# Two transformer blocks on one core: the second block's first layer, its context rows taken out of the joint output product and feed-forward

## The chip, the cores and the metric

The kernel runs on one core of a Trainium2 chip. The metric is device time in microseconds (us) of one execution, as the median of several. TensorE does the matrix products, VectorE and ScalarE work on tiles in SBUF and PSUM, GpSimd on tiles in SBUF, SyncE (SP) issues the DMA transfers.

## The reference, cut to what matters

Two blocks follow each other on 256 rows of 1024 values. The change lies in the second block. It has two layers; in each, 256 latent rows `x` attend to latents and context, and in the first layer alone the 256 context rows `xc` attend to themselves and get an output product and a feed-forward of their own, with the same weights:

```python
    for l in range(DEPTH):
        last = l == DEPTH - 1
...
        y = _merge(o_lat[0], o_lat[1], o_lat[2], lam, lam_init, g_diff_sub[l]) @ w_out[l]
        x = x + gt_a * _rms(y, g_attn_post[l])
        if not last:
            o_ctx = [_sdpa(qc, kc, vc, s) for (qc, kc, vc), s in zip(cxt, scales)]
            yc = _merge(o_ctx[0], o_ctx[1], o_ctx[2], lam, lam_init, g_diff_sub[l]) @ w_out[l]
            xc = xc + cgt_a * _rms(yc, g_attn_post[l])
        hf = _rms(x, g_ffn_pre[l]) * (1.0 + sc_f) + sh_f
        x = x + gt_f * _rms(_swiglu(hf, w_ffn_gate[l], w_ffn_up[l], w_ffn_down[l]), g_ffn_post[l])
        if not last:
            hfc = _rms(xc, g_ffn_pre[l]) * (1.0 + csc_f) + csh_f
            xc = xc + cgt_f * _rms(_swiglu(hfc, w_ffn_gate[l], w_ffn_up[l], w_ffn_down[l]), g_ffn_post[l])
```

The shifts, scales and gates (`sh_a` and so on, the modulation) come from a product of a condition vector with `w_ada[l]`, 24 MB a layer. The second layer needs `xc` only for its keys and values. w_out is 1024x1024, gate and up 1024x2816, down 2816x1024, all in 32 bits.

## The kernel before

**Products.** Every weight goes through `Stream.chunk` (L187 to 208): a load of 1 MB on SP's queue into one of three raw buffers (`wraw`), then in two pieces a rounded copy by ScalarE (`whi`, L204) and what is missing from it (`wlo`, L206), by the engines listed in `s.low` in turn: VectorE alone, or VectorE and GpSimd where the code sets it so. A pair (`whi`, `wlo`) lies in one of two or three pairs of buffers (`s.parts(n)`). The rows are split in the same way, and a product is three matmuls: rounded rows with rounded weights, the rows' low part with rounded weights, rounded rows with the weights' low part. `Stream.tform` (L242) holds the weight stationary and moves the rows; `Stream.nat` and `Stream.tile` (L211, L229) hold 128 rows stationary and move up to 512 weight columns.

**The second block's first layer** (`second`, L2028). The context's projections come first. Then the context's attention runs with the latents' projections as steps beside it (`attention(0, qc, ...)`, with `every` 2 and three PSUM banks for the projections). Then the latents' attention: `attend` (L1619) makes 20 units, each a generator with several steps, and `pipelined` runs them in 26 rounds: pack keys and queries, scores, maximum (VectorE) and exponential (ScalarE), transposes of the weights, product with the values, normalising, transposing back into `m`. It has five PSUM banks for scores and transposes and two for outputs. Before every round, `self.fill("attention 0")` does one step of the modulation (`ada`, L1377: load 1 MB, four matmuls of 32 columns by 512 at L1390, or a step that sorts a finished block); `FILL` (L18) says how many steps are done where. The second layer's modulation, 27 steps with 24 loads, all runs here.

Then `out2` (L1957) and `ffn2` (L1974) take two jobs, latents and context, with seven banks. In the output product and the down product each weight chunk serves four row tiles, in gate and up it moves 512 columns: both jobs' rows. `closing` (L1866) ends each: square sums (L1882), gate (L1884), inverse roots on [128, 1] (`row_rstd`, L387 to 406), sum into `x` or `xc` (L1891), new roots. `mod_norm` and `norm_T` (L1426, L445) turn the rows for the next product: a diagonal of roots (L413), matmuls (L456), scale and shift on VectorE and ScalarE (L465, L466), low parts (L468). `xc` is stored to DRAM (`xcd`, L2099) and loaded again (L2110) for the second layer's projections, whose query products need only `x`.

**Order.** The program's order is only a priority: the build (`schedule_with_timeline_sim=True`) orders each engine's instructions by its own estimate of when they can start.

## Time and profile before

| | us |
|---|---|
| median of 3 runs | 2714.01 |
| lowest, highest run | 2701.88, 2716.73 |
| the profiled execution | 2723.91 |
| its span | 2722.1 |
| its mean granted TensorE clock | 0.966 |

The profile is of one execution, a little slower than the median. Its page gives the busy share of each engine over the span and in 40 slices of 68 us; stretches of the span can be read one by one, with the busy time of each engine, the mean granted clock of TensorE (1.00 is 2.4 GHz, 0.5 is 1.2 GHz) and the mean busy share of the DMA engines. The second block's first layer begins about 1590, the latents' attention 1728, output product 1834, feed-forward 1904, second layer 2268, its attention 2384, its feed-forward 2528. A matmul's duration overlaps its neighbours'; the pace is the distance from start to start.

### The profile page before, as it was taken

To read this page: it belongs to the slowest core of one execution; us is meant where nothing else is said; L and a number is where in the kernel's file an instruction comes from. 1 tells how busy PE (TensorE), PEld (TensorE's weight loads), DVE (VectorE), ACT (ScalarE), POOL (GpSimd) and SP (SyncE) were. 2 spreads that over 40 slices of the span, in tenths; PEclk is the share of its full clock that TensorE was granted. 3 is DMA by queue.
4 is the path that set the end of the run, shared out by engine and by line. 5 is a ranking of instruction groups with operands and counts; after the bars stand their busy time and mean duration, and the time that the engine had idled before them with its cause. 6 is when DMAs were issued, how large, how long until landed. Compare 5 with 4: busy or idle time off the path is not lost. (4 is left out here: it accounts for less than half of the span.)

```text
span 2722.1 us, 38616 instructions
## 1 busy us (share of the span) xinstructions
PE 2612.3 (96%) x15079; PEld 2170.8 (80%) x15079; DVE 1857.5 (68%) x3078; ACT 1503.8 (55%) x2273; POOL 226.5 (8%) x306
## 2 busy tenths in 40 slices
PE   9999999999999999999999889998999997998998
PEld 7789889688888888887888688567888886866997
DVE  5755466688888989888999778476333336674654
ACT  5344355477777777777777545464422223373543
POOL 1000022100000000000000113012000004310000
PEclk9999999999999999999999998899999997987999
DMA  7755574589999999999999732561322332310553
GB/s 238 278 186 186 171 242 140 201 320 358 346 346 349 360 343 358 366 350 361 350 347 362 243 113 90 202 217 55 101 93 93 103 99 64 112 32 32 171 171 124
DMA packets 305645, 590.21 MB, mean 217 GB/s; under 512 B 16196, under 2 KB 118322, under 8 KB 299186
## 3 DMA queue, kind: packets, MB, share of 16 engines
q1 hardware_dynamic: 305458, 587.69, 62.0%
q8 instruction: 120, 1.97, 0.3%
q14 instruction: 67, 0.55, 0.1%
HBM read 584.49 MB, written 3.16 MB: 216 GB/s over the span
## 5 line engine op out<-in xcount | busy, mean ns | idle before, releaser
L206 DVE TENSOR_TENSOR wlo<-wraw,whi 128x1024 fp32r<-128x1024 f32 (+2 forms) x974 | 1126.3, 1203 | 404.4 <-ACT whi L204 378.8
L204 ACT ACTIVATE whi<-wraw 128x1024 fp32r<-128x1024 f32 (+3 forms) x1023 | 990.8, 1032 | 428.0 <-PE bank L238 165.7
L237 PE MATMUL bank<-whi,xe 128*128 128x512 f32 x896 | 356.5, 398 | 1.1 <-ACT whi L204 1.1
L238 PE MATMUL bank<-whi,xe 128*128 128x512 f32 x896 | 353.3, 394 | 0.0
L240 PE MATMUL bank<-wlo,xe 128*128 128x512 f32 x896 | 254.5, 398 | 1.2 <-DVE wlo L206 1.1
L252 PE MATMUL bank<-fhTl,whi 128*128 128x256 f32 (+1 forms) x736 | 226.3, 331 | 1.9 <-POOL fhTl L468 1.9
L251 PE MATMUL bank<-fhTh,whi 128*128 128x256 f32 (+1 forms) x736 | 226.0, 331 | 2.2 <-ACT fhTh L466 2.2
L237 PEld LDWEIGHTS bank<-whi,xe 128*128 128x128 f32 x896 | 168.6, 188 | 42.9 <-ACT whi L204 2.3
L240 PEld LDWEIGHTS bank<-wlo,xe 128*128 128x128 f32 x896 | 166.8, 189 | 41.2 <-DVE wlo L206 4.2
L238 PEld LDWEIGHTS bank<-whi,xe 128*128 128x128 f32 x896 | 169.1, 189 | 37.7
L1217 PE MATMUL my<-whi,fl 128*128 128x512 f32 x448 | 174.7, 391 | 0.0
L1216 PE MATMUL my<-whi,fh 128*128 128x512 f32 x448 | 174.1, 392 | 0.2 <-ACT fh L349 0.2
L206 POOL TENSOR_TENSOR wlo<-wraw,whi 128x1024 fp32r<-128x1024 f32 (+3 forms) x49 | 108.2, 2220 | 606.5 <-PE bank L254 323.7
L252 PEld LDWEIGHTS bank<-fhTl,whi 128*128 128x128 f32 x736 | 138.7, 190 | 15.9 <-POOL fhTl L468 3.4
L251 PEld LDWEIGHTS bank<-fhTh,whi 128*128 128x128 f32 x736 | 138.3, 190 | 16.2 <-ACT fhTh L466 3.7
L254 PE MATMUL bank<-fhTh,wlo 128*128 128x256 f32 (+1 forms) x736 | 137.9, 330 | 0.0
L238 PE MATMUL bank<-whi,ffl 128*128 128x512 f32 x352 | 137.0, 389 | 0.0
L237 PE MATMUL bank<-whi,ffh 128*128 128x512 f32 x352 | 136.7, 389 | 0.0
L1219 PE MATMUL my<-wlo,fh 128*128 128x512 f32 x448 | 133.9, 396 | 0.0
L254 PEld LDWEIGHTS bank<-fhTh,wlo 128*128 128x128 f32 x736 | 114.5, 191 | 12.5
L252 PE MATMUL bank<-hTl,whi 128*128 128x256 f32 (+1 forms) x424 | 108.0, 291 | 2.7 <-DVE hTl L462 2.2
L251 PE MATMUL bank<-hTh,whi 128*128 128x256 f32 (+1 forms) x424 | 108.5, 292 | 2.1 <-ACT hTh L461 2.1
(602 smaller groups left out, 4454.4 us busy)
## 6 DMA issues: line engine op xcount, KB each, us to landing
wraw<-in_odd_exp_w_dram SPq DMA_DIRECT2D x334, 1024.0 KB, 6.9
wraw<-in_w_ada_dram SPq DMA_DIRECT2D x48, 1024.0 KB, 6.3
wraw<-in_even_ffn_w_dram SPq DMA_DIRECT2D x32, 1024.0 KB, 5.1
wraw<-in_w_ffn_gate_dram SPq DMA_DIRECT2D x22, 1024.0 KB, 5.6
wraw<-in_w_ffn_up_dram SPq DMA_DIRECT2D x22, 1024.0 KB, 5.2
wraw<-in_w_ffn_down_dram SPq DMA_DIRECT2D x20, 1024.0 KB, 4.9
wraw<-in_w_in_dram SPq DMA_DIRECT2D x18, 1024.0 KB, 5.4
wraw<-in_odd_w_in_dram SPq DMA_DIRECT2D x16, 1024.0 KB, 6.7
```

The source lines that it names most:

```text
L204: self.k.behind(0, nc.scalar.activation(h[:, at], r[:, at], AF.Copy))
L206: last = eng.tensor_sub(l[:, at], r[:, at], h[:, at])
L237: nc.tensor.matmul(o, xh[:, k0 + k, ts], h[:, k], start=k0 + k == 0, stop=False)
L238: nc.tensor.matmul(o, xl[:, k0 + k, ts], h[:, k], start=False, stop=False)
L240: nc.tensor.matmul(o, xh[:, k0 + k, ts], l[:, k], start=False, stop=k0 + k == K - 1)
L251: nc.tensor.matmul(outs[g], h[:, k, cs], xh[:, k], start=k == 0, stop=False)
L252: nc.tensor.matmul(outs[g], h[:, k, cs], xl[:, k], start=False, stop=False)
L254: nc.tensor.matmul(outs[g], l[:, k, cs], xh[:, k], start=False, stop=k == K - 1)
L1216: nc.tensor.matmul(y[half], fh[:, r0 + r], h[:, r, hs], start=c + r == 0, stop=False)
L1217: nc.tensor.matmul(y[half], fl[:, r0 + r], h[:, r, hs], start=False, stop=False)
L1219: nc.tensor.matmul(y[half], fh[:, r0 + r], l[:, r, hs], start=False, stop=c + r == F // 128 - 1)
```

## The change

The context's output product, closing, norm and feed-forward become a generator of 33 steps, `context_rest`, with chunks of their own: each of these weights is now loaded and split once for the latents and once for the context. Before two of three rounds of the latents' attention one step is made (17 in all), four more behind the latents' output product, the rest behind the latents' feed-forward. The context's matmuls have three PSUM banks of their own from the latents' attention on; that attention keeps three and one for outputs, and every fourth time the modulation's bank; the latents' output product and feed-forward have four. In the context's steps GpSimd takes every other low part. Some tiles of the attention have a buffer less (`tight`), and in the latents' feed-forward two pairs of split buffers are left of three.

The modulation of the second layer leaves the latents' attention: two of its steps go with each of the context's column groups that are done after that attention (14 steps), 13 behind the second layer's attention. `attend` can write its output as a rounded copy and a low part (`put`), which the context's and the second layer's attention do; the second layer's attention leaves the modulation's bank alone. `closing`, `out2` and `ffn2` are written for one job. The context's rows are stored to `xcd` twice (after the output product and at the end), and loaded again for the second sum.

```diff
-    "even norm": 0, "even": 1, "even out": 3, "even ffn norm": 3, "even ffn": 0, "odd norm": 3, "odd": 0, "before router": 0, "router": 7, "norm 01": 0, "norm 00": 0, "latents 0": 0, "attention 0": 1, "out 0": 1, "ffn norm 0": 0, "ffn 0": 0, "layer 1": 0, "norm 10": 0, "norm 11": 0, "latents 1": 0, "out 1": 0, "ffn norm 1": 0, "ffn 1": 0, "end": 0,
+    "even norm": 0, "even": 1, "even out": 3, "even ffn norm": 3, "even ffn": 0, "odd norm": 3, "odd": 0, "before router": 0, "router": 7, "norm 01": 0, "norm 00": 0, "out 0": 0, "ffn norm 0": 0, "ffn 0": 0, "context": 0, "rest of context": 2, "layer 1": 0, "norm 10": 0, "norm 11": 0, "attention 1": 0, "ffn norm 1": 0, "ffn 1": 0, "end": 0,
...
-                    m = self.apool.tile([128, 512], F32, name="m4", bufs=2)
+                    m = self.apool.tile([128, 512], F32, name="m4", bufs=1)
...
-    def attend(self, pool, ps, pp, l, q, kvs, m, beside=None, shared_bank=True):
+    def attend(self, pool, ps, pp, l, q, kvs, m, beside=None, share=6, tight=False):
...
-            if shared_bank and turn[1] % 6 == 0:
+            if share and turn[1] % share == 0:
...
+        def put(k, o, scale=1.0):
+            if not isinstance(m, tuple):
+                nc.scalar.activation(m[:, k], o, AF.Copy, scale=scale)
+                return
+            hi, lo = (z[:, k] for z in m)
+            nc.scalar.activation(hi, o, AF.Copy, scale=scale)
+            nc.vector.scalar_tensor_tensor(lo, o, scale, hi, op0=OP.mult, op1=OP.subtract)
...
-            p = pool.tile([128, 2, nk], F32, name="ap", bufs=4 if nkc == 4 else 5)
+            p = pool.tile([128, 2, nk], F32, name="ap", bufs=5 if nkc < 4 else 3 if tight else 4)
...
-            return pool.tile([128, nkc, T], F32, name="apt", bufs=3)
+            return pool.tile([128, nkc, T], F32, name="apt", bufs=2 if tight else 3)
...
-            nc.scalar.activation(m[:, at + pr], back(on, b), AF.Copy)
+            put(at + pr, back(on, b))
...
-    def closing(self, s, pool, jobs, l, j, store=None):
+    def closing(self, s, pool, x, n, l, j, store=None):
...
+    def gated(self, z, gate, o, junk, ss, c, t):
+        cs = slice(c * 512, (c + 1) * 512)
+        self.nc.scalar.activation(junk, o, AF.Square, accum_out=ss[:, c, t:t + 1])
+        self.nc.vector.tensor_mul(z[:, cs], o, gate[:, cs])
+    def context_rest(self, s, hold, m, out):
+        nc, tc = self.nc, self.tc
+        F = 2816
+        ctx_in = self.i["ctx_2"][0].rearrange("(t p) d -> p t d", p=128)
+        halves = [slice(c * 512, (c + 1) * 512) for c in range(2)]
+        def added(x, ys, ss, junks):
+            r, new = self.row_rstd(ss), self.stats()
+            for t in range(NT):
+                for c, cs in enumerate(halves):
+                    nc.vector.scalar_tensor_tensor(x[:, t, cs], ys[t][:, cs], r[:, t:t + 1], x[:, t, cs],
+                                                   op0=OP.mult, op1=OP.add)
+                    nc.scalar.activation(junks(), x[:, t, cs], AF.Square, accum_out=new[:, c, t:t + 1])
+            nc.sync.dma_start(out, x)
+            return self.row_rstd(new)
+        with tc.tile_pool(reuse_waits="tile", name="cx1", bufs=1, side="right") as pool:
+            xc = pool.tile([128, NT, D], F32, name="cxx")
+            nc.sync.dma_start(xc, ctx_in)
+            gate = self.gate_rows(s, pool.tile([128, D], F32, name="cgate"), 0, 0, 1)
+            w = self.wview(self.dram("w_out_2", 0))
+            ys = [pool.tile([128, D], F32, name="cy", bufs=NT) for _ in range(NT)]
+            ss = self.stats()
+            junk = lambda: pool.tile([128, 512], F32, name="sqj", bufs=1)
+            for c in range(2):
+                banks = [s.bank() for _ in range(NT)]
+                for k0 in range(0, KD, 4):
+                    chunk = s.chunk(w[:, k0:k0 + 4, halves[c]])
+                    for x, o in zip(tiles(m), banks):
+                        s.tile(o, x, chunk, k0, KD)
+                    yield
+                for t, o in enumerate(banks):
+                    self.gated(ys[t], gate, o, junk(), ss, c, t)
+            r = added(xc, ys, ss, junk)
+            hT = self.packs(hold, "c")
+            exhaust(self.mod_norm(s, pool, xc, r, hT, self.g["g_ffn_pre"][0], 0, 1, 1, "cy"))
+            yield
+        w1, w3, w2 = (self.wview(self.dram(f"w_ffn_{a}_2", 0)) for a in ("gate", "up", "down"))
+        with tc.tile_pool(reuse_waits="tile", name="cx2", bufs=1, side="right") as pool:
+            ys = [pool.tile([128, D], F32, name="cy", bufs=NT) for _ in range(NT)]
+            ff, done = [], 0
+            def down(group, evacuate):
+                nonlocal done
+                k = 2 * len(group)
+                xs = tiles([Cat([z[a] for z in group], 0) for a in range(2)])
+                for c, cs in enumerate(halves):
+                    for t, o in enumerate(s.nat(xs, w2[:, done:done + k], c * 512, 512)):
+                        evacuate(ys[t], c, t, o)
+                done += k
+            def summed(y, c, t, o):
+                z = y[:, halves[c]]
+                if done:
+                    nc.vector.tensor_add(z, z, o)
+                else:
+                    nc.scalar.activation(z, o, AF.Copy)
+            for f0 in range(0, F, 256):
+                z = [pool.tile([128, 2, T], F32R, name=a, bufs=3) for a in ("cfh", "cfl")]
+                a, b = banks = [s.bank() for _ in range(2)]
+                for o, w in zip(banks, (w1, w3)):
+                    s.tform([(hT, [o[:, :T], o[:, T:]])], w, f0, 256)
+                    yield
+                sg = pool.tile([128, 2, T], F32, name="ffs", bufs=1)
+                flat = sg.rearrange("p g n -> p (g n)")
+                nc.scalar.activation(flat, a, AF.Silu)
+                nc.vector.tensor_mul(flat, flat, b)
+                self.split(*z, sg)
+                self.fill("rest of context" if self.late else "context")
+                ff.append(z)
+                m = 2 if done else 1
+                if len(ff) > m:
+                    down(ff[:m], summed)
+                    ff = ff[m:]
+                    yield
+            xc = hold.tile([128, NT, D], F32, name="ch")
+            nc.sync.dma_start(xc, out)
+            z = hold.tile([128, 4, 512], F32, name="cl")
+            gate = self.gate_rows(s, z[:, :2].rearrange("p a n -> p (a n)"), 0, 1, 1)
+            ss = self.stats()
+            turn = [0]
+            def junk():
+                turn[0] += 1
+                return z[:, 2 + turn[0] % 2]
+            def last(y, c, t, o):
+                summed(y, c, t, o)
+                self.gated(y, gate, y[:, halves[c]], junk(), ss, c, t)
+            down(ff, last)
+            yield
+            self.context_rms = added(xc, ys, ss, junk)
...
+            ff = self.packs(pool, "ff", F // 128)
+            self.ffn_up(s, pool, hT, w1, w3, ff, 0, F, f"ffn {l}", [norm()])
+            self.fill("end", ADA * (l + 1))
+            return self.closing(s, closed, x, 0, l, 1, store)(ff, w2)
...
-        def attention(l, q, kvs, m, beside=None, every=0, banks=0, steps=None):
-            if not steps:
-                self.fill("end", -(-self.filled // (ADA // 3)) * (ADA // 3))
+        def attention(l, q, kvs, m, project=None, every=0, banks=0, po=2, **more):
             with (tc.tile_pool(reuse_waits="tile", name="att", bufs=1) as pool,
-                  tc.tile_pool(reuse_waits="tile", name="attps", bufs=5 - banks, space=PSUM) as ps,
-                  tc.tile_pool(reuse_waits="tile", name="attpo", bufs=2, space=PSUM) as pp, ExitStack() as more):
-                if not beside:
-                    return self.attend(pool, ps, pp, l, q, kvs, m, steps and (lambda: self.fill(steps)), not steps)
-                more.enter_context(s.banks(banks))
-                s.low = [nc.vector, nc.gpsimd]
-                count = iter(range(1, 100))
-                self.attend(pool, ps, pp, l, q, kvs, m, lambda: next(count) % every == 0 and next(beside, None))
-                exhaust(beside)
-                s.low = [nc.vector]
+                  tc.tile_pool(reuse_waits="tile", name="attps", bufs=7 - banks - po, space=PSUM) as ps,
+                  tc.tile_pool(reuse_waits="tile", name="attpo", bufs=po, space=PSUM) as pp):
+                if not project:
+                    return self.attend(pool, ps, pp, l, q, kvs, m, **more)
+                with s.banks(banks):
+                    s.low = [nc.vector, nc.gpsimd]
+                    count = iter(range(1, 100))
+                    self.attend(pool, ps, pp, l, q, kvs, m, lambda: next(count) % every == 0 and next(project, None),
+                                **more)
+                    exhaust(project)
+                    s.low = [nc.vector]
...
-                    mc = mix.enter_context(tc.tile_pool(reuse_waits="tile", name="mix", bufs=1, side="right")).tile(
-                        [128, KD, T], F32, name="mc")
+                    hold = mix.enter_context(tc.tile_pool(reuse_waits="tile", name="hold", bufs=1, side="right"))
+                    mc = self.packs(hold, "c")
                     with tc.tile_pool(reuse_waits="tile", name="projl", bufs=1) as pool:
                         q = lp.tile([128, NT, self.QW], F32, name="q0")
-                        attention(0, qc, [kv[1]], mc, self.project(s, pool, 0, [(hl, True, kv[0], q)], tabs), 2, 3)
-                m = mix.enter_context(tc.tile_pool(reuse_waits="tile", name="mixl", bufs=1, side="right")).tile(
-                    [128, KD, T], F32, name="m")
-                self.fill("latents 0", 2 * ADA // 3)
-                attention(0, q, kv, m, steps="attention 0")
-            with s.parts(1), s.banks(7), tc.tile_pool(reuse_waits="tile", name="xcp", bufs=1) as xp:
-                xc = xp.tile([128, NT, D], F32, name="xc")
-                nc.sync.dma_start(xc, rows(ctx_in))
-                stats = self.out2(s, xp, [(x, 0, m), (xc, 1, mc)], 0)
-                self.fill("out 0", ADA)
-                stats = self.ffn2(s, xp, [(x, 0), (xc, 1)], stats, 0)
-                nc.sync.dma_start(rows(xcd), xc)
+                        attention(0, qc, [kv[1]], mc, self.project(s, pool, 0, [(hl, True, kv[0], q)], tabs), 2, 3,
+                                  tight=True)
+                banks = mix.enter_context(tc.tile_pool(reuse_waits="tile", name="cbk", bufs=3, space=PSUM))
+                rest = self.context_rest(s, hold, mc, rows(xcd))
+                def context(n):
+                    before, s.psum = s.psum, banks
+                    s.low = [nc.vector, nc.gpsimd]
+                    for _ in range(n):
+                        next(rest, None)
+                    s.psum, s.low = before, [nc.vector]
+                with tc.tile_pool(reuse_waits="tile", name="mixl", bufs=1) as mp:
+                    m = mp.tile([128, KD, T], F32, name="m")
+                    self.late = False
+                    rounds = iter(range(100))
+                    attention(0, q, kv, m, banks=3, po=1, share=4, tight=True,
+                              beside=lambda: context(1 if next(rounds) % 3 else 0))
+                    with s.banks(4), tc.tile_pool(reuse_waits="tile", name="cl", bufs=1) as closed:
+                        r = self.out2(s, closed, x, m, 0, False)
+                        self.late = True
+                        context(4)
+            with s.banks(4), tc.tile_pool(reuse_waits="tile", name="cl", bufs=1) as closed:
+                r = self.ffn2(s, closed, x, r, 0)
+                context(99)
         self.fill("layer 1", ADA + ADA // 3)
...
-                    pre(s, pool, xc, stats[1], h[1], 1, 1)
+                    pre(s, pool, xc, self.context_rms, h[1], 1, 1)
...
-                self.fill("latents 1", ADA + 2 * ADA // 3)
-                attention(1, q, kv, m)
+                attention(1, q, kv, m, share=0)
+                self.fill("attention 1", 2 * ADA)
```

## Rows read from the trace of the kernel before

**Rows 1.** The page: the core's busy line, and the clock in 40 slices.

```profile
PE 2612.3 (96%) x15079; PEld 2170.8 (80%) x15079; DVE 1857.5 (68%) x3078; ACT 1503.8 (55%) x2273; POOL 226.5 (8%) x306
...
PEclk9999999999999999999999998899999997987999
```

**Rows 2.** Busy time in stretches; the columns stand in the first line.

```profile
core 0: us, PE busy (x) PEld busy (x) DVE busy (x) ACT busy (x) POOL busy (x), PEclk, DMA share, GB/s
1728.00:1834.00 106.00, 103.06 (x1006) 62.32 (x1003) 65.08 (x157) 63.60 (x150) 13.97 (x54) 0.98 0.63 231
1880.00:1912.00 32.00, 22.41 (x126) 19.59 (x125) 23.75 (x79) 14.00 (x30) 7.52 (x7) 0.79 0.10 34
1904.00:2268.00 364.00, 363.96 (x1709) 305.81 (x1710) 140.17 (x184) 107.73 (x148) 14.79 (x12) 1.00 0.29 94
2264.00:2312.00 48.00, 28.37 (x127) 24.57 (x126) 35.94 (x121) 19.75 (x41) 19.15 (x12) 0.69 0.20 65
2384.00:2485.00 101.00, 94.91 (x825) 67.92 (x826) 62.26 (x148) 59.26 (x146) 13.39 (x54) 0.76 0.07 22
2528.00:2714.00 186.00, 185.31 (x1308) 174.44 (x1307) 98.19 (x125) 85.04 (x120) 0.52 (x1) 1.00 0.51 165
...
2428.00:2476.00 48.00, 48.00 (x261) 31.52 (x262) 20.88 (x56) 18.34 (x45) 5.82 (x25) 0.51 0.00 1
2272.00:2280.00 8.00, 0.00 (x0) 0.00 (x0) 8.00 (x8) 2.22 (x4) 7.06 (x3) 0.68 0.17 49
```

**Rows 3.** TensorE in order of time, joint feed-forward: ends of two groups of 24.

```profile
2235.14 1.98 PE L254 MATMUL bank<-fhTh,wlo 128*128 128x512 f32 x8
...
2240.58 1.98 PE L254 MATMUL bank<-fhTh,wlo 128*128 128x512 f32 x8
```

**Rows 4.** The chain of waits, second layer's feed-forward: start, length, what.

```profile
2530.03 0.96 PE bank L254 x8
...
2532.91 0.96 PE bank L254 x8
```

**Rows 5.** Instructions by line and shape, 1650 to the end: split pieces.

```profile
L206 DVE TENSOR_TENSOR wlo<-wraw,whi 128x1024 fp32r<-128x1024 f32 x143 | 169.0, 1220 | 156.6 <-ACT whi L204 156.6
L204 ACT ACTIVATE whi<-wraw 128x1024 fp32r<-128x1024 f32 x158 | 158.3, 1051 | 199.1 <-PE bank L252 74.7 <-PE bank L238 66.4 <-issue 52.8
...
L206 POOL TENSOR_TENSOR wlo<-wraw,whi 128x1024 fp32r<-128x1024 f32 x15 | 37.0, 2489 | 398.8 <-PE bank L254 323.7 <-ACT whi L204 75.0
```

**Rows 6.** One line, 1700 to 1834: the modulation's matmuls.

```profile
L1390 PE MATMUL aps<-wraw,cp x192: 592/592/1063, 1718.0 to 1804.1; 128*32 128x512 f32 x192
```

**Rows 7.** TensorE in order of time: one modulation chunk, and products with the identity.

```profile
1724.59 1.07 PE L1390 MATMUL aps<-wraw,cp 128*32 128x512 f32 x8
1725.58 1.15 PE L1693 MATMUL po<-kv,apt 128*64 128x64 f32 x32
...
1835.34 2.94 PE L1421 MATMUL bank<-consts,mod 128*128 128x128 f32 x24 [0.21 <-ACT m L1737]
```

**Rows 8.** The chain of waits, last down product: two groups of 12.

```profile
2661.03 0.91 PE bank L240 x4
...
2663.76 0.91 PE bank L240 x4
```

**Rows 9.** VectorE and GpSimd in order of time, second joint.

```profile
2266.65 0.15 DVE L395 TENSOR_TENSOR ss<-ss 128x1 f32<-128x1 f32 x1
...
2274.95 2.30 DVE L395 TENSOR_TENSOR ss<-ss 128x1 f32<-128x1 f32 x1
2277.17 2.38 DVE L403 SCALAR_TENSOR_TENSOR rstdb<-rstd,rstdv 128x1 f32<-128x1 f32 x1
...
2273.77 5.76 POOL L206 TENSOR_TENSOR wlo<-wraw,whi 128x1024 fp32r<-128x1024 f32 x2
```

**Rows 10.** ScalarE in order of time: the table load ahead of silu.

```profile
1925.10 1.28 ACT L512 ACT_TABLE_LOAD   x1
```

**Rows 11.** Busy time, a stretch of the context's attention beside the latents' projections.

```profile
1664.00:1704.00 40.00, 39.72 (x286) 32.20 (x285) 31.08 (x107) 19.97 (x58) 17.27 (x44) 1.00 0.28 96
```

**Rows 12.** Waits of SP's queue, 2262 to 2320: total, times, longest.

```profile
SPq L2099 <- DVE rstd L399: 9.3, 1, 9.3
...
SPq L2110 <- DMA xcd<-xc: 3.6, 1, 3.6
```

177 lines of the change are left out of this document (55 added, 122 removed).

## The prediction, made before the changed kernel was run

> **What bounds the kernel now.** I read the profile's page first. TensorE is busy 96% of the span and the clock line stands at 9 in nearly every slice [rows 1], so the time is TensorE's work plus the places where it waits or runs at the lower clock. The dips of the clock line lie in the second block, so I then read stage by stage (busy time in stretches). There a stretch's length less busy time times granted clock is what TensorE lost. In the joint feed-forward, 1904 to 2268, it loses nothing (363.96 of 364 us at 1.00) [rows 2]. Between output product and feed-forward it loses 32 - 22.41 x 0.79 = 14.3 us, between feed-forward and the second layer's projections 48 - 28.37 x 0.69 = 28.4 us; one 8 us stretch there has no matmul at all while VectorE is busy for all of it [rows 2]. In the latents' attention (1728 to 1834) it loses 106 - 103.06 x 0.98 = 5.0 us, in the second layer's attention 101 - 94.91 x 0.76 = 28.9 us, most of it from 48 us at clock 0.51, about the 1.2 GHz level [rows 2].
>
> So the two joints are chains of small VectorE, ScalarE and GpSimd steps that all latents and all context rows go through at once, with no matmul left to do. The change puts the context's matmuls there, and into the first layer's attention.
>
> **The change, part by part.** Most of it moves work that TensorE must do anyway; only differences count.
>
> *Narrower products.* Gate and up are computed with the weight stationary. Joint, 24 matmuls of 512 columns take 2240.58 - 2235.14 = 5.44 us [rows 3]. Alone, 24 of 256 columns take 2532.91 - 2530.03 = 2.88 us [rows 4]. There are 22 groups of 128 columns in each of two weights: 44 x (2 x 2.88 - 5.44) = **+14.1 us** on the path. Output and down products have the rows stationary and 512 weight columns moving, one product per row tile before and after: 0.
>
> *Weights loaded and split twice.* w_out is 4 chunks of 1 MB, gate, up and down 11 each: 37 more chunks, each with two more ScalarE pieces (1.05 us) and two low parts, on VectorE 1.22 us or GpSimd 2.49 us [rows 5]. That is 74 x 1.05 = 78 us ScalarE, 37 x 1.22 = 45 us VectorE, 37 x 2.49 = 92 us GpSimd, spread over some 400 us of stages in which these engines are busy 4 to 61% of the time and the DMA engines 29 to 63% [rows 2]. Cover: TensorE's 5.4 to 5.8 us per chunk; if it were gone, a chunk would wait about 3.3 us (two ScalarE pieces, one VectorE piece). 37 more issues stand on SP's queue, and 0 is taken. The latents' feed-forward also loses its third pair of split buffers: a pair comes free in the second half of its chunk, and the next but one needs it a whole chunk later, 5.8 us against 3.3; 0.
>
> *What stands in the latents' attention.* The layer-1 modulation leaves it: 192 records of two passes, four matmuls a chunk, are 24 chunks [rows 6]; one takes 1725.58 - 1724.59 = 1.0 us [rows 7]. So 106 us hold 24 of modulation and 82 of attention and stalls. In come 17 of the context's 33 steps (26 rounds, two of three): output product 8 x 12 matmuls at 2.72/12 us [rows 8] = 21.8 us, norm and gate 40 x 2.94/24 [rows 7] = 4.9, ten weight chunks at 2 x 2.88 = 57.6, the down product of three groups 72 x 2.72/12 = 16.3: 101 us. The stage should take 82 + 101 = 183 us, every us of which leaves a later stage. What mixing costs I have to bound. Below: it hides the stage's 5.0 us of losses. Above: the low parts that GpSimd takes hold VectorE. While GpSimd did two such pieces (5.76 us), VectorE operations of 128x1 took 2.30 and 2.38 us, where the same took 0.15 [rows 9]. Eighteen chunks in the attention bring some 17 full pieces, 17 x 2.49 = 42 us, and the attention's chain runs through VectorE (maxima, reciprocals). Silu among exponentials adds up to 8 table loads of 1.28 us [rows 10]: 10 us. So -5 to +52. Nearest is the stretch where the latents' projections run beside the context's attention with GpSimd on low parts too: 17.27 us of GpSimd in 40, TensorE at 39.72, clock 1.00 [rows 11]. By it nearly all is hidden; for its 3 (not 5) score banks, one output bank and the table loads I take **+5 us**.
> The Trainium skill (ScalarE: Activation LUTs, Rules for kernel authors) says to do all work of one table set before switching, and prices a switch with its drain at about 2.7 us; by that price, were all eight on the path, the term would be 21 us, and the whole 16 us later. Rows 10 show the load alone, 1.28 us; no row shows a drain.
>
> *First joint.* Four context steps follow the latents' output product: three weight chunks, a down product of two groups and four modulation steps, 3 x 5.76 + 10.9 + 4 = 32 us of matmuls against 14.3 lost. The closing chain also has two row tiles instead of four. Bounds 0 and -14.3; **-12**, since the chain's own first matmuls still wait.
>
> *Second joint.* After the latents' last down product 12 steps remain: nine weight chunks and three down products of two groups, 9 x 5.76 + 3 x 10.9 = 84.5 us, and ten modulation steps. Under them the latents' closing and the layer-1 norm of x run. That norm now waits for the modulation's first block, which is filled in with the context's ninth group; 4 x 5.76 + 2 x 10.9 = 45 us of matmuls stand behind that. What is late next is the context's own end: four evacuations, two inverse roots, the sum, store and reload of xcd, norm. The reload queues on SP behind the store, and weights of the projections behind both; before, SP waited 9.3 us for the store's data and 3.6 us for the store [rows 12]. (xcd is now stored and reloaded once more, in the attention and ahead of the context's last down product; there loads queue behind those waits at the same price, under the latents' matmuls: 0.) The cover of the context's end is the latents' query products, which need only x: the rank-256 product (5.8 us), 48 matmuls of 512 columns (10.9) and 60 narrower ones (8): 25 us. So I leave 6 us: **-22 us**, bounds 0 and -28.4.
>
> *Modulation.* Fourteen of its 27 steps run in the context's later steps, 13 (11 chunks) after attention 1, where the build may pull them in. Out of the first layer: **-11 us**. In attention 1 they cost between +11 (all on the path) and 11 - 28.9 = -18 (all hidden, clock kept at 2.4 GHz). The nearest row is the latents' attention with 24 such chunks, at clock 0.98 [rows 2]; but 11 placed late need not keep it: **0**. The rest (merged copies, `sc` and `m4` with one buffer less, packs written directly) comes to under 1 us either way.
>
> Sum: 14.1 + 0 + 5 - 12 - 22 - 11 + 0 = -25.9 us. The profiled execution took 2723.9 us (span 2722.1 and 1.8 around it), 9.9 above the median 2714.0. It would become 2698; against the median, **2688 us**.
>
> **Rivals.** (a) *More is hidden.* The mix hides the stage's own losses (-10 against my +5), the second joint closes fully (-6, the first -2), and attention 1 keeps its clock, say -10: 2660 us. For: rows 11 and the latents' attention at 0.98 in rows 2. Against: the build orders each queue by its own estimate of time, and what comes late holds what stands behind it.
> (b) *The context's end takes the second joint's place.* If its chain of roots, store, reload and norm starts when the x-only products are already spent, the 22 us stay: 2710 us, no difference to be told. For: the chain is as long as the one that now leaves 8 us without a matmul [rows 2]. Against: 25 us of x-only products.
> (c) *Slower: VectorE is held in the attention.* The place is the latents' attention; the price is 42 us of held VectorE and 10 of table loads instead of my 5: 2688 + 47 = 2735 us. It decides from 45 of those 52 us on, that is if nearly every GpSimd piece falls on the maximum, exponential, transpose chain. For: rows 9, and VectorE's 65 us there plus 21 of new low parts and 42 held make 128 of 183, before the context's norm, evacuations and sums. Against: rows 11.
> The Trainium skill (GPSIMD Engine Reference, Key points) warns of this: GpSimd shares its SBUF interfaces with VectorE and contends with instructions that have two SBUF inputs. Rows 9 agree.
>
> **How the numbers follow.** Forecast 0.51 (own range 2674 to 2700), (a) 0.19, (b) 0.19, (c) 0.11. A measurement of this kernel can tell about 0.5%, 13.6 us, so faster means below 2700.4 and slower above 2727.6. Faster is forecast and (a), 0.70; same is (b), 0.19; slower is (c), 0.11. The range takes in most of (a) and (b), leaves (c) out and the far end of (a): 2658 to 2718.
>
> **What would show it.** Right: the stretch of the latents' attention 183 to 190 us at clock near 1; 11 chunks of modulation in attention 1; no stretch of 8 us without a matmul between the latents' last down product and attention 1; latents' feed-forward at 186 us, as the second layer's is now [rows 2]. Wrong: long VectorE entries beside GpSimd low parts with TensorE waiting on the maxima (c); TensorE waiting on the context's roots or on the reload (b); a latents' feed-forward above 190 us, which would mean that two pairs of buffers or the second loading are not free.

## The result, and the profile after

The changed kernel takes 2747.6 us (median of 4 runs, 2743.8 to 2748.6), the kernel before 2715.4 beside it: ratio 1.0123, 95% interval 1.0084 to 1.0163. It is 32 us slower where 26 us faster were forecast; 2747.6 lies outside the range. The profiled execution after took 2748.1 us (span 2746.3), that of before 2723.9, so the two traces show 24 of the 32 us.

The page's busy line and clock line after, which answer to [rows 1]:

```profile
PE 2628.8 (96%) x16039; PEld 2223.0 (81%) x16039; DVE 1926.6 (70%) x3120; ACT 1578.7 (57%) x2359; POOL 301.0 (11%) x326
...
PEclk9999999999999999999999997899999997987999
```

TensorE is as busy as before, with 960 matmuls more, and the clock line dips in the same three places. The stretches after, columns as in [rows 2]:

```profile
1728.00:1923.00 195.00, 187.90 (x1605) 157.17 (x1600) 120.21 (x239) 121.36 (x232) 58.52 (x74) 0.96 0.30 98
1945.00:1983.00 38.00, 37.60 (x262) 31.38 (x261) 30.96 (x74) 19.79 (x34) 16.80 (x9) 1.00 0.72 249
1983.00:2168.00 185.00, 185.00 (x1321) 175.18 (x1320) 94.52 (x112) 84.11 (x117) 0.00 (x0) 1.00 0.58 188
2171.00:2271.00 100.00, 98.36 (x673) 83.47 (x671) 55.62 (x85) 42.89 (x58) 37.05 (x16) 1.00 0.76 256
2268.00:2316.00 48.00, 22.14 (x94) 18.18 (x92) 28.41 (x77) 16.24 (x31) 15.08 (x10) 0.64 0.36 112
2272.00:2280.00 8.00, 0.00 (x0) 0.00 (x0) 7.71 (x7) 3.23 (x6) 7.17 (x4) 0.69 0.68 221
2280.00:2288.00 8.00, 0.00 (x0) 0.00 (x0) 6.91 (x24) 2.72 (x8) 1.72 (x1) 0.50 0.11 40
2392.00:2508.00 116.00, 108.78 (x933) 71.38 (x932) 71.31 (x167) 65.90 (x152) 14.75 (x56) 0.79 0.35 128
```

In their order: the latents' attention with the context's steps in it; the first joint, now full; the latents' feed-forward, full; the rest of the context's feed-forward, nearly full; the second joint, which has two stretches of 8 us without a matmul where [rows 2] have one; the second layer's attention, 15 us longer and still at a low clock. The two joints had been the aim: one is closed, the other is wider than before.

TensorE's waits from the context's last product to the second layer's attention, after (total, times, longest):

```profile
PE bank L456 <- DVE ndg L413: 18.9, 1, 18.9
PE bank L1508 <- ACT sc L1499: 7.7, 2, 6.1
PE bank L252 <- DVE h0l L468: 2.9, 1, 2.9
```

The longest of them before the change, between the feed-forward and the second layer's attention:

```profile
PE bank L456 <- DVE ndg L413: 15.4, 2, 14.7
```

L456 turns `x` for the second layer, with the scaled identity `ndg`. So the wait that was to go has become longer. After, the roots of `x` stood at 2184.6 and the modulation's first block at 2202, 87 us before `ndg`. VectorE in order of time shows where `ndg` stood:

```profile
2277.14 2.30 DVE L395 TENSOR_TENSOR ss<-ss 128x2 f32<-128x2 f32 x1
2279.48 2.27 DVE L397 TENSOR_SCALAR rstdv<-ss 128x2 f32<-128x2 f32 x1
...
2283.57 2.74 DVE L1949 SCALAR_TENSOR_TENSOR ch<-cy,rstd,ch 128x512 f32<-128x512 f32 x4
...
2289.40 0.47 DVE L413 TENSOR_SCALAR ndg<-consts,rstd 128x128 f32<-128x128 f32 x2
```

It stands behind the context's whole closing: gates, first roots, sum (L1949), second roots. So what was to be done under the context's matmuls began only when they and their closing were over.

For the experiments I cut each trace into five stages: A from the end of the latents' first-layer projections to their output product (the latents' attention), B from there to their feed-forward (output product, first joint), C to its last down product, D to the end of the second layer's projections (rest of the context, second joint, projections), E to the second layer's feed-forward. Stage lengths are differences of matmul times of the one profiled execution.

| kernel | median us | ratio to before, interval | A | B | C | D | E |
|---|---|---|---|---|---|---|---|
| before | | | 139.3 | 58.0 | 373.7 | 113.1 | 138.5 |
| after | 2747.6 | 1.0123 (1.0084 to 1.0163) | 231.6 | 59.2 | 188.6 | 221.2 | 152.5 |
| e1 | 2737.8 | 1.0108 (1.0075 to 1.0142) | 232.0 | 59.5 | 188.5 | 218.4 | 145.8 |
| e2 | 2730.0 | 1.0068 (1.0044 to 1.0091) | 225.3 | 58.3 | 188.8 | 218.2 | 145.2 |
| e3 | 2747.2 | 1.0127 (1.0083 to 1.0171) | 231.6 | 59.2 | 188.5 | 221.6 | 152.1 |
| e4 | 2743.5 | 1.0104 (1.0058 to 1.0150) | 260.7 | 59.4 | 192.3 | 204.4 | 142.2 |
| e5 | 2737.2 | 1.0079 (1.0052 to 1.0106) | 232.0 | 59.8 | 188.6 | 214.1 | 152.2 |
| e6 | 2729.4 | 1.0049 (1.0028 to 1.0070) | 225.4 | 58.2 | 188.9 | 211.8 | 151.7 |
| e7 | 2729.0 | 1.0052 (1.0034 to 1.0070) | 232.1 | 60.1 | 188.6 | 220.7 | 135.4 |
| e8 | 2755.3 | 1.0147 (1.0109 to 1.0184) | +30.6 | 60.0 | 188.6 | 213.7 | 135.7 |
| e9 | 2735.2 | 1.0078 (1.0057 to 1.0099) | 231.7 | 59.6 | 188.6 | 222.1 | 143.8 |
| e10 | 2735.8 | 1.0076 (1.0059 to 1.0093) | 230.2 | 59.8 | 188.5 | 211.1 | 143.8 |
| e11 | 2707.8 | 0.9969 (0.9954 to 0.9985) | 225.3 | 58.3 | 188.9 | 208.5 | 134.4 |
| e12 | 2701.2 | 0.9954 (0.9936 to 0.9971) | 225.3 | 58.3 | 188.9 | 201.0 | 132.7 |
| e13 | 2730.2 | 1.0067 (1.0039 to 1.0095) | 229.4 | 59.1 | 188.5 | 220.8 | 135.0 |
| e14 | 2708.0 | 0.9997 (0.9972 to 1.0022) | 230.1 | 58.3 | 188.9 | 198.6 | 139.3 |
| e15 | 2771.7 | 1.0235 (1.0182 to 1.0289) | 132.6 | 49.9 | 192.3 | 360.0 | 149.4 |
| e16 | 2695.0 | 0.9933 (0.9913 to 0.9953) | 224.8 | 58.3 | 188.9 | 201.0 | 133.0 |

(e8: its A begins inside work that was moved; +30.6 is how much later its output product starts than after's, 1953.9 against 1923.3.)

### The profile page after: what moved, and what is told of

It reads as the page before. It is cut to its first block, busy times and chain, and to the rows that moved or that the text cites. A ratio compares the mean times of both kernels' runs of the same rounds, so it can differ in the third digit from the quotient of the medians.

```text
span 2746.3 us, 40908 instructions
## 1 busy us (share of the span) xinstructions
PE 2628.8 (96%) x16039; PEld 2223.0 (81%) x16039; DVE 1926.6 (70%) x3120; ACT 1578.7 (57%) x2359; POOL 301.0 (11%) x326
## 5 line engine op out<-in xcount | busy, mean ns | idle before, releaser
L206 DVE TENSOR_TENSOR wlo<-wraw,whi 128x1024 fp32r<-128x1024 f32 (+2 forms) x1014 | 1187.1, 1216 | 419.7 <-ACT whi L204 387.2
L204 ACT ACTIVATE whi<-wraw 128x1024 fp32r<-128x1024 f32 (+3 forms) x1099 | 1065.8, 1032 | 441.3 <-PE bank L238 172.0
L206 POOL TENSOR_TENSOR wlo<-wraw,whi 128x1024 fp32r<-128x1024 f32 (+3 forms) x85 | 201.7, 2379 | 600.9 <-ACT whi L204 375.7
L252 PE MATMUL bank<-fhTl,whi 128*128 128x256 f32 x704 | 173.0, 284 | 0.9 <-POOL fhTl L468 0.9
L251 PE MATMUL bank<-fhTh,whi 128*128 128x256 f32 x704 | 172.8, 284 | 0.7 <-ACT fhTh L466 0.7
L237 PE MATMUL bank<-whi,ffh 128*128 128x512 f32 x264 | 102.9, 390 | 0.0
L238 PE MATMUL bank<-whi,ffl 128*128 128x512 f32 x264 | 102.7, 389 | 0.0
L254 PE MATMUL bank<-fhTh,wlo 128*128 128x256 f32 x704 | 100.2, 285 | 0.0
```

Of the source, the lines that this page charges most:

```text
L204: self.k.behind(0, nc.scalar.activation(h[:, at], r[:, at], AF.Copy))
L206: last = eng.tensor_sub(l[:, at], r[:, at], h[:, at])
L237: nc.tensor.matmul(o, xh[:, k0 + k, ts], h[:, k], start=k0 + k == 0, stop=False)
L238: nc.tensor.matmul(o, xl[:, k0 + k, ts], h[:, k], start=False, stop=False)
L251: nc.tensor.matmul(outs[g], h[:, k, cs], xh[:, k], start=k == 0, stop=False)
L252: nc.tensor.matmul(outs[g], h[:, k, cs], xl[:, k], start=False, stop=False)
```

## The experiments

**e1: x's norm with scratch of its own.** `xs` is a pool opened ahead of the layer's `proj`:

```diff
-                    pre(s, pool, x, r, h[0], 1, 0)
+                    pre(s, xs, x, r, h[0], 1, 0)
...
-                    tabs = self.tables(pool, 1)
+                    tabs = self.tables(xs, 1)
```

> The scratch of the second layer's norm of x (scaled identity, gains, copies) and its tables get memory of their own instead of memory that the context's sum still reads; nothing else is changed. Theory M (shared memory made x's norm wait for the context's end): the 18.9 us wait of TensorE on the scaled identity behind the context's last down product falls under 4 us, the joint loses 15 to 25 us less, and the ratio to before falls from 1.012 to 1.003 to 1.007 (2722 to 2733 us). Rival E (the context's own end is the chain that decides): the wait only moves to the context's norm behind the query products; total within 6 us of 2747. Rival G (VectorE held by GpSimd's low parts): the scaled identity comes earlier on its queue, but VectorE entries of 2 us stand in its chain all the same; under 8 us won.

TensorE's waits in that part of e1, then VectorE in order of time:

```profile
PE bank L1508 <- ACT sc L1499: 7.7, 2, 6.1
PE bank L251 <- ACT h0h L466: 7.4, 5, 5.9
PE bank L456 <- DVE cy L1993: 4.2, 1, 4.2
PE bank L252 <- DVE h0l L468: 4.0, 1, 4.0
```

```profile
2293.49 0.17 DVE L1429 SCALAR_TENSOR_TENSOR mg<-mod,cols 128x8 f32<-128x8 f32 x1 [1.82 <-DMA xcd<-ch]
2293.57 0.47 DVE L413 TENSOR_SCALAR ndg<-consts,rstd 128x128 f32<-128x128 f32 x2
2293.97 0.41 DVE L468 TENSOR_TENSOR h0l<-xf,h0h 128x256 fp32r<-128x256 f32 x1
```

The 18.9 us wait is gone, so memory had held it: nothing but the place of the scratch was changed. But D is only 2.8 us shorter. The norm's matmuls next wait 4.2 us for a bank that the context's sum still reads (L1993); then `x`'s first low part `h0l` stands in VectorE's queue behind the context's closing, the store of `xcd` and the gains of the context's norm. The wait had three holders, one behind the other, and all three theories had a part; the other 7 us of the 10 are in E (last section).

**e2: no low parts on GpSimd in the context's steps.**

```diff
-                    s.low = [nc.vector, nc.gpsimd]
+                    s.low = [nc.vector]
```
(in `context`)

> The context's weights have all low parts on VectorE, none on GpSimd, in the latents' attention and behind it. Rival G (GpSimd's pieces hold VectorE at the context's end and in the attention): the 2.3 us entries there go, the second joint is 8 to 15 us shorter, ratio 1.006 or less. Theory M: the wait on the scaled identity stays at 13 to 19 us, since only the two holds of some 2 us go; VectorE has some 18 pieces of 1.2 us more in the attention, so the total lies between 5 us less and 10 us more than 2747.

The wait on the scaled identity stays (18.2 us from the context's last product to `x`'s norm), as theory M said; the total fell by more than it allowed. A is 6.3 us shorter, B 0.9, D 3.0, E 7.3. In E nothing was changed; there the stretch at 1.2 GHz is 23.9 us instead of 41.0. e6 against e5 gives the price without that: A 6.6, B 1.6, D 2.3, E 0.5; medians 7.8 us. So GpSimd's pieces cost the change 8 to 10 us, some 6.5 of them in the latents' attention, although VectorE has the more to do without them. The maxima of that attention, which read PSUM, take as long beside these pieces as without them; first after, then in e2 (count, duration in ns, first and last start):

```profile
L1671 DVE TENSOR_REDUCE ast<-sbank x32: 669/688/693, 1740.9 to 1890.8; 128x1 f32<-128x512 f32 x32
```

```profile
L1671 DVE TENSOR_REDUCE ast<-sbank x32: 675/682/692, 1732.1 to 1879.7; 128x1 f32<-128x512 f32 x32
```

Some other VectorE operations in stage A are longer after than in e2; line by line, their mean durations times their counts differ by some 16 us in all, a third of it in VectorE's own low parts (mean 1.46 us against 1.17).

**e3 and e7: the modulation of the second layer's attention, later.** e3 fills one step a round from the ninth on; e7 orders each step behind the last value product as well:

```diff
-                attention(1, q, kv, m, share=0)
-                self.fill("attention 1", 2 * ADA)
+                late = iter(range(100))
+                def step():
+                    if next(late) >= 8:
+                        self.ada_after = self.recent
+                        self.fill("attention 1")
+                        self.ada_after = None
+                attention(1, q, kv, m, share=0, beside=step)
+                self.fill("end", 2 * ADA)
```
(e7; `self.recent` is the last matmul of `weigh`; e3 is without the two `ada_after` lines)

> The modulation steps that stood behind the second layer's attention, and were pulled to its start, stand one in each round from the ninth on. Theory C (they cost their full 11 us because they stand where TensorE is busy, ahead of the stretch at 1.2 GHz): now they fill that stretch; the second layer's attention falls from 116 us to 103 to 109, the 41 us at 1.2 GHz get shorter by at least 15, total 7 to 13 us below 2747. Rival W (they cost what they take wherever they stand, the stretch's clock does not hear of them): attention 114 to 120 us, total within 4 us of 2747, or above it if each chunk takes 2 us at 1.2 GHz.

> e3 left each instruction where it had been; here each modulation step from the ninth round of the second layer's attention on is ordered behind the last value product recorded so far, so that it can't be pulled to the start. Theory C: the stretch at 1.2 GHz in that attention falls from 41 us to 25 or less and the attention from 116 to 104 to 110 us, ratio 1.008 to 1.010. Rival W: 114 to 120 us, ratio 1.011 to 1.014.

e3 tells nothing: the build, for which the program's order is a priority only, put the chunks where they had been. The modulation's matmuls in that attention, after and in e7 (count, duration in ns, first and last start):

```profile
L1390 PE MATMUL aps<-wraw,cp x88: 592/592/618, 2392.2 to 2426.9; 128*32 128x512 f32 x88
```

```profile
L1390 PE MATMUL aps<-wraw,cp x88: 592/612/1062, 2419.7 to 2474.9; 128*32 128x512 f32 x88
```

And that attention in e7 as a stretch, up to its last value product, which answers to the last stretch after:

```profile
2393.00:2492.00 99.00, 93.94 (x936) 60.87 (x935) 70.27 (x168) 66.07 (x152) 13.64 (x56) 0.98 0.44 150
```

The same 11 chunks, 27 to 48 us later: the clock is 0.98 instead of 0.79, the attention takes 99 us instead of 116, E 135.4 instead of 152.5, the median falls by 18.6. E is then shorter than before the change, where it held no chunk (138.5). Theory C holds, and more strongly than it had said. Not all of the 17 us is the chunks' place: e9 and e10, whose edits lie elsewhere, have E at 143.8 with less time at 1.2 GHz (last section), and against them e7 gains 8 us.

**e4, e8, e13: the modulation in the first layer.** e4 puts all 27 steps into the latents' attention again, e8 18 of them into the context's attention; both take the modulation's bank from the scores (`share=0`). e13 puts nine steps between the two attentions and gives up no bank:

```diff
                     m = mp.tile([128, KD, T], F32, name="m")
+                    self.fill("end", ADA + ADA // 3)
                     self.late = False
```

> All 27 modulation steps of the second layer stand in the latents' attention again, one a round, as before the change; the attention gives up the modulation's bank for its scores. Theory C: the second layer's attention is back at 101 to 104 us, the context's rest at 93 to 95, the latents' attention about 24 longer less 6 to 10 that its own idle places give back; total 10 to 18 us below 2747. Rival W (the places in the latents' attention are full with the context's steps): attention longer by 24 or more, total within 5 us of 2747.

> 18 of the 27 modulation steps stand, ordered in the same way, two a round from the sixth round of the context's own attention on (which gives up the modulation's bank for scores), the other nine in the context's rest, none in the second layer's attention. Theory S (the context's attention lost its cover when the modulation left its end: 30.7 us at 1.2 GHz from 1695, 10.2 us before the change): that stretch falls to 15 us or less, the second layer's attention to 100 to 106 us, and the latents' attention starts less than 12 us later than now; total 8 to 18 us below 2747, ratio 1.006 to 1.009. Rival W: 18 chunks cost 16 us or more in their new place, total within 4 us of 2747.

> The changed kernel with the nine steps of the modulation's first block of the second layer (eight chunks) between the context's and the latents' attention, where modulation stood before the change; three chunks are left behind the second layer's attention. Theory S (with the modulation went the cover of that place, 30.7 us at 1.2 GHz from 1695 against 10.2 before): the stretch falls to 20 us or less, from the end of the latents' projections to their output product it takes 229 to 234 us (231.6 now) though eight chunks more are in it, and the second layer's attention is 8 us shorter; ratio 1.008 to 1.010. Rival W (eight chunks cost eight us there too): 238 to 241 us in that part, ratio 1.011 to 1.014.

e4: A is 29.1 us longer with 24 chunks in it, C 3.7, D and E are 27 shorter, and the median falls by 4: rival W. With no chunk in the second layer's attention, E is 142.2. e8: the output product starts 30.6 us later with 16 chunks; TensorE waits 6.8 us for a score bank at the start, and the total is 8 us above after, where neither theory had it. That fewer score banks eat up what the place gains is likely, but no run varies the banks alone. e13 leaves the banks as they are. The stretch with the start of the latents' attention after, then in e13:

```profile
1690.00:1730.00 40.00, 36.08 (x239) 25.65 (x236) 26.07 (x83) 19.25 (x57) 9.91 (x21) 0.62 0.22 79
```

```profile
1690.00:1730.00 40.00, 38.11 (x307) 25.03 (x308) 19.75 (x71) 14.48 (x46) 3.19 (x14) 0.70 0.31 122
```

The 1.2 GHz stretch there is 23.9 us instead of 30.7, and A is 2.2 us shorter with eight chunks more. Eight chunks that elsewhere take 8 us cost nothing here: theory S, a little weaker in the clock than it said (e14, below, is less kind to it). (The median falls by 17 us. In the profiled execution, the trace of which is 23.5 us shorter, 17.5 of them are E's, with three chunks left and 20.5 us at 1.2 GHz; the others lie between 2722.6 and 2741.0.)

**e15: no context step in the latents' attention** (`beside` left out, all 33 steps behind it).

> The changed kernel with no context step in the latents' attention: all 33 behind it (four in the first joint, the rest behind the latents' feed-forward), modulation steps with the same groups as before. Theory X (mixing is worth what the attention loses without it): the attention alone is 82 us of matmuls and loses 20 to 30 us at 1.2 GHz and in waits, the rest of the context takes 101 us more; total 10 to 22 us above 2747. Rival G (the attention pays for the mix in held VectorE and table loads what it gains): total within 5 us of 2747.

The stretch of the latents' attention in e15:

```profile
1690.00:1820.00 130.00, 118.19 (x1101) 85.36 (x1102) 84.67 (x224) 75.80 (x197) 16.57 (x68) 0.86 0.08 26
```

The kernel is 24 us slower than after, a little more than theory X said, but not for its reason. Alone the attention takes 132.6 us; with some 101 us of the context's matmuls in it (the prediction's estimate), 231.6: they cost 99 us, so the mix comes nearly free but hides little of the attention's own losses. (Length less busy time times clock says the same: 28.4 us lost in the stretch above, 231 - 220.04 x 0.90 = 33.0 from 1692 to 1923 after.) The 24 us are lost in D, where TensorE now waits twice for a scaled identity:

```profile
PE bank L456 <- DVE ndg L413: 39.2, 2, 20.4
```

The wait of 20.4 us is new. Behind the latents' last down product stands the context's own first closing (roots, sum, new roots, norm), with no matmul ready, and the clock falls to 0.5 in it. In the kernel after, the attention's matmuls cover this chain. So this is what the mix wins, and it is the part of the change that works. A second reading: alone, without a chunk, A takes 132.6; before the change it took 139.3 with 24 chunks. The modulation had cost some 7 us there, not 24 (the banks differ, so this is rough).

**e5, e6: x's norm ahead of the context's last steps.** The second layer's tiles are laid out behind the latents' feed-forward, and

```diff
+            with s.banks(4):
+                context(5)
+                self.fill("layer 1", ADA + ADA // 3)
+                pre(s, xs, x, r, h0, 1, 0)
+                tabs = self.tables(xs, 1)
+                context(99)
```

> The second layer's norm of x and its tables stand in the program five context steps behind the latents' feed-forward, ahead of the context's last steps, with scratch and banks of their own; the layer's tiles are laid out before the context ends. Theory O (the wait has three holders, one behind the other: the shared scratch, which the first experiment took away, the banks that the context's last products hold, and the place on VectorE's queue behind the context's closing): all are gone, so no matmul waits on the scaled identity of x or on its copies behind the context's last product; from that product to the second layer's attention some 98 to 104 us instead of 121, ratio to before 1.001 to 1.005. Rival E (the context's own end is longer than the products that need x alone): the wait comes back behind the query products, 108 to 115 us, ratio 1.007 to 1.010.

> As e5, and the context's low parts all on VectorE as in e2. If the two prices are separate (GpSimd's pieces cost the latents' attention some 6 us, the order of the norms the joint), the ratio is that of e5 less 0.004 to 0.007, 0.995 to 1.001; if they are one price seen twice, it is that of e5 within 0.002.

TensorE's longest waits from the context's last product on, e5:

```profile
PE bank L1508 <- ACT sc L1499: 13.3, 2, 7.2
PE bank L456 <- DMA xc<-xcd: 6.2, 1, 6.2
PE bank L251 <- DVE cy L1993: 4.2, 1, 4.2
```

Rival E for the most part. `x`'s norm waits for nothing, D is 7.1 us shorter, but 28 us now lie between the context's last product (2277.1) and its own norm (2304.9). In that time the rank-256 product runs (8 us); the next matmul on TensorE's queue (L1508) needs that product's square, which stands on ScalarE behind the squares of the context's sum. The other x-only products stand behind L1508. e6 is 7.8 us below e5, a little under the forecast for separate prices; by the stages they are separate, since A, B and D are 10.5 us shorter, as in e2 against after (10.2).

**e9, e10: what is left of the joint.** e9 gives `sc` six buffers in the second layer; e10 is e5 with `xc` kept in a tile of `xs`, without the last store and the reload.

> The changed kernel with six instead of five buffers of the projections' scratch (sc) in the second layer alone. Theory B (the ring is why TensorE waits 6.1 us for the square of the rank-128 product and 1.6 us for that of the rank-256 one): these waits fall to under 4 us together, ratio 1.009 to 1.011. Rival Q (the square stands behind other work on ScalarE's and VectorE's queues, whatever its buffer): waits and time unchanged, ratio 1.011 to 1.014.

> As e5, and the context's rows stay on the chip for the second layer's norm: no last store, no reload. In e5 the reload landed 6.2 us after TensorE was free for the context's norm. Theory E (what is left of the joint is the context's own end, 28 us from its last product to its norm, of which the x-only products cover 8): the reload is the last link of that chain, its 4 to 6 us go, ratio that of e5 less 0.0015 to 0.0025. Rival Q (VectorE's queue ends the chain, the reload lands beside it): under 2 us won.

e9: the two waits on the squares fall from 7.7 to 3.5 us, as theory B said, and D does not get shorter (222.1): other waits take their place. The 12 us of the median are E again, with 20.5 us at 1.2 GHz. e10: D is 3.0 us shorter than in e5 and the median 1.4. The wait of 6.2 us on the reload is gone, but the one on the square (L1508) grows from 13.3 to 19.8: half of what the reload had cost was in line behind VectorE and ScalarE anyway, nearer to rival Q than to theory E.

**e11, e12, e14, e16: the parts together.** e11 is e5 with e2, e7 and e9; e12 adds e10; e14 adds e13 to e12; e16 shares the low parts of the second layer's projections between VectorE and GpSimd in e12.

> x's norm first, low parts on VectorE, modulation pinned late in the second layer's attention, six scratch buffers. If the prices add up (10 us for x's norm, 8 to 10 for the low parts, 18 for the modulation, 0 to 4 for the buffer): 2706 to 2714 us, ratio 0.996 to 1.000. If they overlap: 2716 to 2724 us.

> As e11, with the context's rows kept on the chip as in e10: 4 to 6 us below e11 by theory E, the same within 2 us by rival Q.

> e12 with the same nine steps between the two attentions. By theory S 3 to 8 us below e12 (2693 to 2698), by rival W 2701 or a few us above, since the second layer's attention then has only three chunks left to keep its clock up with.

> e12 with the low parts of the second layer's projections shared between VectorE and GpSimd, where GpSimd alone made them. If GpSimd's pieces hold the context's closing on VectorE in the second joint: 2 to 6 us below e12. If VectorE has no room there: 0 to 4 us above.

The prices add up: 40 us below after for e11, 46 for e12, whose D is 20.2 and E 19.8 us shorter. Keeping the rows is worth 7.5 us of D here (e12 against e11), more than the 3.0 of e10. With the waits on the rows' end gone (L456 <- L413 1.0 us in e12), what is left is the square and a bank:

```profile
PE bank L1508 <- ACT sc L1499: 11.3, 2, 9.5
PE bank L251 <- DVE cy L1995: 4.5, 1, 4.5
PE bank L456 <- DVE ndg L413: 1.0, 1, 1.0
```

e14 is 6.7 us slower than e12: most of its modulation is spent when the second layer's attention comes (37.5 us at 1.2 GHz there, E 6.6 longer), and A is 4.8 us longer with the same eight chunks that had cost e13 nothing. So theory S holds for e13 and not here. e16 equals e12 in every stage within 0.5 us; its lower median came from another chip's runs and lies outside these stages, so it is not the edit's. e11, e12 and e16 are a little faster than the kernel before (0.9969, 0.9954 and 0.9933, intervals below 1): with its arrangement mended, the change pays. In the traces E is 5.8 us shorter in e12 than before the change, and there tied modulation might have helped the kernel before as well; that was not run.

## Why the prediction was wrong

The traces differ by 24.2 us, the forecast for this execution by -25.9: 50.1 us. Two stages hold it. D was forecast as 113.1 + 94.5 - 22 = 185.6 and took 221.2 (+35.6); E as 138.5 and took 152.5 (+14.0). Together 49.6. A came out 10.3 longer than forecast (139.3 + 188 - 106 = 221.3), and a profile that reached A 7.1 us earlier, with B, C and the end, gives that back. The last 10 us to the median are the correction from a profiled execution to the median, which the profile after did not need (2748.1 against 2747.6).

*Second joint, -22: the step that failed most.* "Under them the latents' closing and the layer-1 norm of x run." The closing did; the norm did not. I had followed what the norm needs as data (`x`, its roots, the modulation) and found 45 us of matmuls behind it. I had not asked which tiles and banks it is written into, nor what stands ahead of it on VectorE's queue. e1 and e5 show the three holders. "25 us of x-only products" failed too: of these one runs (8 us), since the next stands behind a square on a queue that the context's closing fills. Of the 35.6 us, 5.2 are the rest of the context (99.7 against 94.5), 30.4 the joint with the projections (121.5 against 113.1 - 22). The 48 us around it lose 48 - 22.14 x 0.64 = 33.8 us, where [rows 2] lose 28.4. Rival (b) named this chain, but priced it as no worse than before; it was worse, because x's norm came in line behind the context's end where before both ended together.

*Modulation, -11 and 0.* Between the bounds (-18 to +11) 0 was taken, by the row of the latents' attention, which ran at 0.98 with 24 chunks. There the chunks had been spread over 86 us [rows 6]; the new ones were pulled into the first 35 us, ahead of the stretch that needed them. So the bound "+11, all on the path" is what came: e4, with no chunk there and the same 41.0 us at 1.2 GHz, has E at 142.2, and the 10.3 us from there to 152.5 are the 11 chunks. The other 3.7 of the 14.0 are not theirs, and no run says whose. e7 shows what chunks in place are worth: E 135.4, 3.1 less than before the change, so the 0 would have been nearly right, and the bound of -18 was out of reach. And the 24 us that the chunks were to free in the latents' attention were some 7 (e15): priced at 1.0 us each, they had cost a third of that there or nothing (e13). These 17 us, less 7 by which mixing was better than taken, are the 10.3 of A.

*Mixing, +5.* About -2 by e15 (99 us against an estimate of 101), though GpSimd's pieces cost some 6.5 us there (e2, e6). Rival (c) had the right place at a seventh of its price: the maxima, which its chain needed, are not held at all, and other VectorE operations by some 16 us instead of 42. Silu's eight table loads came as forecast, 1.28 us each, with the next instruction of ScalarE 0.01 us behind the load; no run prices them apart. The Trainium skill (GPSIMD Engine Reference, Key points) speaks of shared SBUF interfaces; the roots at 2.30 and 2.27 us beside GpSimd's pieces, against 0.16 and 0.17 ten us later, agree.

*Right:* the latents' feed-forward, forecast 186, took 185 at full clock with two pairs of split buffers, and the weights' second load and split showed in no wait there; the first joint is full (37.60 of 38 us), 12 of 14.3 us forecast. *Narrower products* fit C, where gate and up took 128 us against 44 x 2.88 = 127. "`sc` with one buffer less: under 1 us" holds for D by e9, where a wait falls and no time is won.

*Slips of the working.* Rival (a)'s terms give 2655 us, not 2660. The 0.15 us set against both operations of [rows 9] is the first one's; the second takes 0.21 us elsewhere in the same joint. Neither bears on the result.

## What to carry to other kernels

Before work is counted as hidden under other work, follow four things, not one: its data, the memory and the banks that it is written into, and its place on every in-order queue that it crosses; a chain freed of one holder is often held by the next, so take them away one after the other and read the wait that remains. Work that depends on nothing is worth most where TensorE would fall to the lower clock, and it must be tied there, since a build that orders by its own estimate may pull it ahead, as here. Price it at what its present place costs, not at its duration.

## What the runs showed of the hardware

The second layer's attention loses a varying time to the clock with its own instructions unchanged: the stretch at 1.2 GHz is 41.0 us after and in e3, e5 and e6, but 27.3 in e1, 23.9 in e2 and e10 and 20.5 in e9, whose edits lie elsewhere, and E follows (152 or 144 to 146 us). Chunks at the start of that attention do not make it: before the change and in e4, with none there, it is 47.8 and 41.0 us. Executions of one kernel differ as much: e10's profiled one took 2722.2 us at mean clock 0.971, its four others 2735.5 to 2738.0 at 0.963 to 0.966. So 7 to 14 us of a total are no verdict on an edit unless the stage that it touches shows them. What decides the length of that stretch was not settled; with modulation tied into it (e7, e11, e12) it nearly vanishes.
